# Latent attention on one core: outputs copied out by ScalarE and added by GpSimd, query blocks in another order

## The chip, the cores and the metric

One core of a Trainium2 chip. Times are device microseconds of one execution; the kernel before took 740.17 us in the median of 3 runs (739.23 to 742.46). One more execution was taken with a profile; all rows of the trace are from it.

## What is computed

One layer for 1024 tokens of width 1024, with 16 heads: multi-head latent attention, a gate on its output, an output projection, then a gated per-layer embedding and a last norm. Cut to what matters here:

```python
u = rmsnorm(x, norm_g) @ w_in            # 384 | 256 | 32 | 1024 columns: c_q, c_kv, k_rope, z
q = rmsnorm(c_q, q_norm) @ w_q_b         # 16 heads of 64 + 32 (rotary)
k_nope, v = split(rmsnorm(c_kv, kv_norm) @ w_kv_b)   # 16 heads of 64 + 64
for blk in range(8):                     # query blocks of 128 tokens
    s = (q_nope @ k_nope.T + rope(q_rope) @ rope(k_rope).T) * scale   # keys up to the block's end
    prob = softmax(where(k_chunk <= q_chunk, s, -inf))                # chunks of 64
    o[blk] = prob @ v
x = x + (o * silu(z)) @ w_out
gate = sigmoid(rmsnorm(x) @ ple_gate)
out = rmsnorm(x + gate * (p @ ple_proj), final_norm)
```

Every product is made of three matmuls of split operands (high x high, high x low, low x high): each operand is stored as a rounded high part and the low part that is left.

## The kernel before, in words

The program is written for a scheduler that orders each engine's instructions ahead of time; on the chip every engine works off its own list in order, and waits at each instruction for what that one needs. The stages:

- Up to 69 us: `u_tile` projects the tokens to the latent queries and keys (`cq_hi`, `cq_lo`, `ckv_hi`, `ckv_lo`).
- 69 to 181 us, the gate projection: the loop over `c` (L500). Each round makes 48 matmuls of `z` for 128 features (L510) from weights that come through the one staging buffer `zs` (`z_weights`, L344: high part `zh` on ScalarE L357, low part `zl` on VectorE L358). Rounds 2 to 5 also project the rotary parts of four heads' queries (`project_r`, L421): 18 matmuls (L417) with `wrh` and `wrl`, the split rotary weights; four products with cosine and sine on VectorE (L429); a copy of the high part on ScalarE (L431); the low part on GpSimd (L432, a subtraction made by the helper `sub_hi`, L91); four DMAs issued by GpSimd (L434). The rotary weights come from `weights_r` (L496), which calls `load_split` (L391): a DMA on SP's queue into one of two buffers `ws`, the high part `hi` (L397) and the low part `lo` (L398, shown as L91), both on GpSimd. The weights of queries, keys and values (`wq`, `wk`, `wv`) go the same way.
- 181 to 517 us, attention, head after head. For each head and query block `scores` (L597) makes the scores in PSUM, masks 64x64 of them (L611), takes the row maximum on VectorE (L613) and the exponential on ScalarE (L618) into `prob`. Blocks over 512 columns use one of two buffers of two banks (`ps_big`), smaller ones one of four buffers of one bank (`ps_tr`), which they share with transposes, projections and outputs. `prob_transposes` (L640) turns the probabilities in TensorE, 128x128 at a time (L118); ScalarE copies the high parts out of PSUM (L656), VectorE the low parts (L657, shown as L91). `values` (L659) multiplies them with the values, once for the blocks 4 to 7 of a head (16 long matmuls' group, `pt1`) and once for the blocks 0 to 3 (`pt0`). The product of the high values stands in one half of the partitions and that of the low values in the other; ScalarE copies one half to `o` (L671), VectorE adds the other half from PSUM (L672), GpSimd multiplies with the gate in `zT` (L674), in the last two heads VectorE.
- The order of the work in attention is a list of head and block (L690); `ORDER` (L37) gives the blocks of a head and `LAST` (L38) those of the last one. The projections of coming heads are put between blocks by tables of positions: `V_FIRST`, `V_AT` for values, `K_AT` for keys, `Q_AT` for queries (L40, L41). Transposes follow 2 blocks behind the scores (`LAG`), outputs 4 (`LAGV`). After each odd head `normalise` (L621) scales the gate by the reciprocal sums. The scheduler makes each engine's list from these positions, so moving one of them moves instructions on all engines.
- From 517 us: output projection and embedding, mostly the matmuls of L757.

Of the kernel before, what the change touches and what calls it, by code (L numbers as in the profile page):

```python
# [9 lines left out]
F32 = mybir.dt.float32  # L10
# [4 lines left out]
ALU = mybir.AluOpType  # L15
AX = mybir.AxisListType

P = 128
# [4 lines left out]
H = 16  # L23
QL = 384
# [9 lines left out]
INV_FREQ = [10000.0 ** (-2.0 * i / ROPE) for i in range(ROPE // 2)]  # L34
HF = ROPE // 2
ROUND = 12582912.0
ORDER = (7, 0, 6, 1, 5, 2, 4, 3)  # L37
LAST = (7, 0, 6, 1, 5, 2, 3, 4)  # L38
WARM = 9
V_FIRST = (1, 1, 5, 3)  # L40
V_AT, K_AT, Q_AT, ROPE_AT = (5, 5, 3, 3), (1, 3), (7, 5), 4  # L41
LAG, LAGV, LEAD, ODD_AT = 2, 4, 2, 1
TWO_PI = 2.0 * math.pi

# [7 lines left out]
def mla_ple_kernel(ctx, tc, x, x_t, p_t, pos, norm_g, w_c, w_z, q_norm, w_q, w_r, kv_norm, w_k, w_v,  # L52
# [7 lines left out]
    V, A, G = nc.vector, nc.scalar, nc.gpsimd  # L60
# [6 lines left out]
    def ps_big():  # L67
        return psum.tile([P, 1024], F32, tag="big", name="ps_big", bufs=2)

    def ps_tr():  # L70
        return psum.tile([P, 512], F32, tag="one", name="ps_tr", bufs=4)
# [18 lines left out]
    def sub_hi(eng, lo, src, hi):  # L90
        eng.tensor_tensor(out=lo, in0=src, in1=hi.bitcast(F32), op=ALU.subtract)  # L91
# [45 lines left out]
    def rh_tile(name):  # L137
        return both.tile([P, S], F32R, tag="rh", name=name, bufs=1)
# [9 lines left out]
    ps = ps_tr()  # L148
# [238 lines left out]
    att1 = late.enter_context(pool("att1", side="right"))  # L387
    att2 = late.enter_context(pool("att2", side="right"))
    k_hi, k_lo = zip(*([att2.tile([P, S], F32R, name=f"k_{z}{e}") for z in ("hi", "lo")] for e in range(2)))

    def load_split(src, cols, name, bufs, home=att1):  # L391
        n = math.prod(cols)
        stg = att1.tile([P, 512], F32, tag="ws", name="ws", bufs=2)[:, :n]
        nc.sync.dma_start(out=stg, in_=src)
        hi = home.tile([P, n], F32R, tag=name + "h", name=name + "h", bufs=bufs)
        lo = home.tile([P, n], F32R, tag=name + "l", name=name + "l", bufs=bufs)
        G.tensor_copy(out=hi, in_=stg)  # L397
        sub_hi(G, lo, stg, hi)  # L398
        return tuple(z.rearrange("p (k n) -> p k n", k=cols[0]) for z in (hi, lo))

    wk_of, wv_of, wq_of, q_of, rq_of = {}, {}, {}, {}, {}
# [91 lines left out]
    zw = zph.enter_context(pool("zw", reuse_waits="tile"))  # L493
    cs = [zw.tile([P, S], F32, name=f"cs{e}") for e in range(2)]

    def weights_r(g):  # L496
        return load_split(w_r[g], (QL // P, P), "wr", 1, zw)


    for c in range(KT):  # L500
# [36 lines left out]
    pt = [[att.tile([P, 16 * g + 10, P], F32R, name=f"pt{g}{z}") for z in "hl"] for g in range(2)]  # L537
    vals = att.tile([P, NT, 2, 4, VD], F32R, name="vals")
    kst = {}

    def prob_tile():
        return att.tile([P, S], F32, tag="prob", name="prob", bufs=3)
# [54 lines left out]
    def scores(h, i):  # L597
        e = h % 2
        q = q_of[h]
        qs = slice(i * P, (i + 1) * P)  # L600
        n = (i + 1) * P
        off = P if n == 640 else 0
        spans = {128: [(0, 256)], 640: [(0, 384), (384, 640)]}.get(
            n, [(a, min(a + 512, n)) for a in range(0, n, 512)])
        ps = ps_big() if n > 512 else ps_tr()
        for s0, s1 in spans:
            for a, b in pairs:
                nc.tensor.matmul(ps[:, off + s0:off + s1], q[a][:, qs], (k_hi, k_lo)[b][e][:, s0:s1],  # L608
                                 start=a + b == 0, stop=a == 1)
        s = ps[:, off:off + n]  # L610
        V.memset(s[0:64, n - 64:], MASKED)  # L611
        mx = small.tile([P, 1], F32, tag="mx", name="mx")
        V.tensor_reduce(out=mx, in_=s, axis=AX.X, op=ALU.max, negate=True)  # L613
        pr = prob_tile()
        if e == 0 and i == order(h)[0]:
            sums[h // 2] = small.tile([P, 2 * NT], F32, tag="l", name="l", bufs=2)
        l = sums[h // 2][:, e * NT + i:e * NT + i + 1]
        A.activation(out=pr[:, :n], in_=s, func=AF.Exp, bias=mx, scale=1.0, accum_out=l)  # L618
        return pr
# [39 lines left out]
    def values(h, g):  # L659
# [9 lines left out]
        top, bot = slice(e * VD, (e + 1) * VD), slice((1 - e) * VD, (2 - e) * VD)  # L669
        o = att.tile([P, 512], F32, tag="o1", name="o1", bufs=2)  # L670
        A.copy(out=o[top], in_=ps[bot])  # L671
        V.tensor_tensor(out=o[top], in0=ps[top], in1=o[top], op=ALU.add)  # L672
        z = zT[top, c, g * 512:(g + 1) * 512]
        (V if h >= H - 2 else G).tensor_tensor(out=z, in0=o[top], in1=z, op=ALU.mult)  # L674

# [226 lines left out]
```

## Time and profile before

| | before |
|---|---|
| runs, median (lowest to highest) | 740.17 us (739.23 to 742.46) |
| the profiled execution | 742.71 us |
| its span, first to last instruction | 740.9 us |
| TensorE busy | 712.6 us (96%) |
| VectorE busy | 525.6 us (71%) |
| ScalarE busy | 401.2 us (54%) |
| GpSimd busy | 209.2 us (28%) |
| granted TensorE clock, mean | 0.989 of full speed |

Time in the trace counts from the span's start. In the profile PE is TensorE, PEld its weight loads, DVE VectorE, ACT ScalarE, POOL GpSimd, SP SyncE, whose queue issues most DMAs. Matmuls overlap, so a matmul's duration is longer than the step from one to the next; the step is the cost. An idle time is put down to what ended it last. `L91` is a helper's line that many subtractions share; the tile names tell them apart.

### The profile page before, as it was taken

The numbers are of one execution on the slowest core, as the hardware profiler recorded it, in microseconds if no ns is written. First come the engines' busy times: TensorE is split into PE (matmuls) and PEld (weight loads), VectorE is DVE, ScalarE is ACT, GpSimd is POOL, SyncE is SP. The second block draws the span as 40 slices with busy tenths as digits, with TensorE's granted clock in tenths as the row PEclk, the third lists the DMA queues.
The fourth block names the chain that finished last, engine by engine and source line by source line (L and its number), as shares of the span: only waits on it lengthen the run. The fifth ranks groups of instructions, "written<-read, shape, count | busy, mean of one in ns | idle before, by whom it ended". The sixth has DMA issues, their size and how long they took to land.

```text
span 740.9 us, 11048 instructions
## 1 busy us (share of the span) xinstructions
PE 712.6 (96%) x3776; PEld 599.2 (81%) x3776; DVE 525.6 (71%) x1270; ACT 401.2 (54%) x921; POOL 209.2 (28%) x204
## 2 busy tenths in 40 slices
PE   8999999979999999999999999999999999999995
PEld 7999888858887778878888788877768887888885
DVE  6995456641887787888788887888555239788854
ACT  6752344331777676777777776776443135243322
POOL 0004316670223232323324232156136132000000
PEclk9999999989999999999999999999999999999998
DMA  8812524462311212101121211033384021110101
GB/s 310 286 56 68 132 77 176 164 216 76 85 44 29 76 30 75 39 27 56 30 75 44 76 29 47 13 115 85 116 297 128 0 86 28 37 43 36 58 28 58
DMA packets 27191, 63.90 MB, mean 86 GB/s; under 512 B 4600, under 2 KB 9088, under 8 KB 27136
## 3 DMA queue, kind: packets, MB, share of 16 engines
q1 hardware_dynamic: 23312, 52.05, 22.6%
q0 software_dynamic: 3536, 11.02, 4.4%
q8 instruction: 30, 0.49, 0.3%
q14 instruction: 25, 0.20, 0.1%
q10 hardware_dynamic: 288, 0.14, 0.1%
HBM read 50.01 MB, written 13.18 MB: 85 GB/s over the span
## 4 chain that ended last, share of the span: by engine, by line
PE 69%; DVE 11%; ACT 8%; issue 4%; DMA 3%; POOL 3%; SPq 0%; ACTq 0%; DVEq 0%; POOLq 0%
PE ps_big L757 17%; PE ps_big L510 9%; PE ps_o L667 9%; PE ps_tr L118 6%; PE ps_big L608 5%; PE ps_pj L417 4%; PE ps_big L212 3%; PE ps_pj L569 3%; PE ps_pj L550 3%; ACT prob L618 3%; DVE pt1l L91 3%; PE ps_pj L757 3%; PE ps_big L213 3%; PE ps_tr L608 2%; DVE mx L613 2%
## 5 line engine op out<-in xcount | busy, mean ns | idle before, releaser
L757 PE MATMUL ps_big<-w,aTh 128*128 128x512 f32 (+1 forms) x480 | 140.2, 392 | 1.8 <-ACT sg L833 1.8
L757 PEld LDWEIGHTS ps_big<-w,aTh 128*128 128x128 f32 x480 | 90.1, 189 | 22.2 <-ACT sg L833 2.2
L118 PE MATMUL ps_tr<-ident,prob 128*128 128x128 f32 x576 | 84.6, 275 | 6.0 <-ACT prob L618 3.3
L757 PE MATMUL ps_big<-w,aTl 128*128 128x512 f32 (+1 forms) x240 | 85.1, 392 | 0.6 <-POOL aTl L91 0.5
L118 PEld LDWEIGHTS ps_tr<-ident,prob 128*128 128x128 f32 x576 | 66.5, 140 | 20.6 <-ACT prob L618 10.2
L674 POOL TENSOR_TENSOR zT<-o,zT 64x512 f32<-64x512 f32 x28 | 36.0, 1287 | 141.2 <-DVE o L672 141.1
L91 DVE TENSOR_TENSOR pt1l<-ps_tr,pt1h 128x512 fp32r<-128x512 f32 (+1 forms) x144 | 72.7, 536 | 3.9 <-ACT pt1h L656 2.5
L656 ACT CAST pt1h<-ps_tr 128x512 fp32r<-128x512 f32 (+1 forms) x144 | 62.0, 470 | 24.2 <-PE ps_tr L118 12.0
L618 ACT ACTIVATE prob<-ps_big,mx 128x1024 f32<-128x1024 f32 (+1 forms) x64 | 61.3, 958 | 18.3 <-DVE mx L613 17.1
L613 DVE TENSOR_REDUCE mx<-ps_big 128x1 f32<-128x1024 f32 (+1 forms) x64 | 64.9, 1015 | 0.3
L358 DVE SCALAR_TENSOR_TENSOR zl<-zs,g_col,zh 128x128 fp32r<-128x128 f32 x56 | 31.3, 607 | 32.9 <-ACT zh L357 32.6
L757 PEld LDWEIGHTS ps_big<-w,aTl 128*128 128x128 f32 x240 | 45.3, 189 | 11.4 <-POOL aTl L91 1.5
L608 PE MATMUL ps_big<-k_hi,qh 128*128 128x512 f32 (+2 forms) x128 | 48.6, 380 | 0.0
L608 PE MATMUL ps_big<-k_hi,ql 128*128 128x512 f32 (+2 forms) x128 | 46.5, 363 | 0.0
L608 PE MATMUL ps_big<-k_lo,qh 128*128 128x512 f32 (+2 forms) x128 | 46.1, 360 | 0.0
L357 ACT ACTIVATE zh<-zs,g_col 128x128 fp32r<-128x128 f32 x56 | 18.3, 392 | 50.2 <-DMA zs<-in_w_z 47.2
L667 PE MATMUL ps_o<-pt1h,vals 128*128 128x512 f32 (+3 forms) x128 | 42.9, 361 | 1.5 <-DVE pt1l L91 1.0
L113 ACT ACTIVATE jk<-xs 128x512 bf16<-128x512 f32 (+2 forms) x25 | 18.7, 750 | 42.3 <-DVE xs L835 35.1
L667 PE MATMUL ps_o<-pt1l,vals 128*128 128x512 f32 (+3 forms) x128 | 41.6, 363 | 0.0
L672 DVE TENSOR_TENSOR o<-ps_o,o 64x512 f32<-64x512 f32 x32 | 22.0, 688 | 25.3 <-ACT o L671 25.2
L618 ACT ACTIVATE prob<-ps_tr,mx 128x128 f32<-128x128 f32 (+1 forms) x64 | 33.8, 529 | 5.5 <-DVE mx L613 5.3
L91 DVE TENSOR_TENSOR pt0l<-ps_tr,pt0h 128x128 fp32r<-128x128 f32 (+2 forms) x80 | 33.2, 416 | 4.5 <-ACT pt0h L656 2.9
(289 smaller groups left out, 1806.7 us busy)
## 6 DMA issues: line engine op xcount, KB each, us to landing
zT<-in_x SPq DMA_DIRECT2D x8, 512.0 KB, 4.5
rlb<-rl SPq DMA_DIRECT2D x32, 128.0 KB, 3.0
wst<-in_w_out SPq DMA_DIRECT2D x8, 512.0 KB, 4.1
xs<-in_x SPq DMA_DIRECT2D x8, 512.0 KB, 7.0
wst<-in_ple_gate SPq DMA_DIRECT2D x8, 512.0 KB, 3.7
zs<-in_w_z SPq DMA_DIRECT2D x14, 256.0 KB, 2.9
out<-xs SPq DMA_DIRECT2D x14, 256.0 KB, 2.0
zT<-in_x_t SPq DMA_DIRECT2D x6, 512.0 KB, 3.7
```

The source lines that it names most:

```text
L91: eng.tensor_tensor(out=lo, in0=src, in1=hi.bitcast(F32), op=ALU.subtract)
L118: nc.tensor.transpose(dst[:, j * P:(j + 1) * P], src[:, j * P:(j + 1) * P], ident)
L358: V.scalar_tensor_tensor(out=lo[:, k, :], in0=stg[:, k, :], scalar=g, in1=hi[:, k, :].bitcast(F32), op0=ALU.mult, op1=ALU.subtract)
L417: nc.tensor.matmul(ps, w[b][:, k, :], (cq_hi, cq_lo)[a][:, k, hf * 512:hf * 512 + 512], start=k == 0 and a + b == 0, stop=k == n - 1 and a ...
L510: nc.tensor.matmul(ps[:, hf * 512:(hf + 1) * 512], wz[b][:, k % 4, :], (hT_hi, hT_lo)[a][:, k, hf * 512:(hf + 1) * 512], start=k == 0 and ...
L608: nc.tensor.matmul(ps[:, off + s0:off + s1], q[a][:, qs], (k_hi, k_lo)[b][e][:, s0:s1], start=a + b == 0, stop=a == 1)
L613: V.tensor_reduce(out=mx, in_=s, axis=AX.X, op=ALU.max, negate=True)
L618: A.activation(out=pr[:, :n], in_=s, func=AF.Exp, bias=mx, scale=1.0, accum_out=l)
L656: A.copy(out=hi, in_=src[:, ks])
L667: nc.tensor.matmul(ps[:, q * P:], vals[:, j, c % 2, 2 * e:2 * e + 2, :], pt[g][n][:, at:at + 4 - q, :], start=j + n == 0, stop=(j, n) == ( ...
L674: (V if h >= H - 2 else G).tensor_tensor(out=z, in0=o[top], in1=z, op=ALU.mult)
L757: nc.tensor.matmul(o, st[a][:, k, :], w[k][b][:, cols], start=k == 0 and a + b == 0, stop=k == nk - 1 and a == 1)
```

## The change

Five edits. `load_split` takes the engine of the high and the low part as arguments, and the rotary weights now use ScalarE and VectorE in place of GpSimd. Scores of 256 to 512 columns use `ps_big` too; only those of 128 columns keep `ps_tr`. In the heads before the last two, ScalarE copies the second half of an output out as well, into a tile `o_hi` of its own, and GpSimd adds the two. The blocks of a head go 7, 6, 0, 1, 5, 4, 2, 3, in the last head 7, 6, 3, 2, 1, 0, 5, 4. The positions of the projections of values, keys and queries are other ones. Behind line 540 the change has one line more than the kernel before (its L609 is L608 there, L614 is L613, L668 is L667), and behind the new adds in `values` six more in all (its L763 is L757).

```diff
@@ -34,11 +34,11 @@
 INV_FREQ = [10000.0 ** (-2.0 * i / ROPE) for i in range(ROPE // 2)]
 HF = ROPE // 2
 ROUND = 12582912.0
-ORDER = (7, 0, 6, 1, 5, 2, 4, 3)
-LAST = (7, 0, 6, 1, 5, 2, 3, 4)
+ORDER = (7, 6, 0, 1, 5, 4, 2, 3)
+LAST = (7, 6, 3, 2, 1, 0, 5, 4)
 WARM = 9
-V_FIRST = (1, 1, 5, 3)
-V_AT, K_AT, Q_AT, ROPE_AT = (5, 5, 3, 3), (1, 3), (7, 5), 4
+V_FIRST = (1, 2, 4, 6)
+V_AT, K_AT, Q_AT, ROPE_AT = (6, 7, 4, 5), (4, 5), (7, 6), 4
 LAG, LAGV, LEAD, ODD_AT = 2, 4, 2, 1
 TWO_PI = 2.0 * math.pi
 
@@ -388,14 +388,14 @@
     att2 = late.enter_context(pool("att2", side="right"))
     k_hi, k_lo = zip(*([att2.tile([P, S], F32R, name=f"k_{z}{e}") for z in ("hi", "lo")] for e in range(2)))
 
-    def load_split(src, cols, name, bufs, home=att1):
+    def load_split(src, cols, name, bufs, home=att1, copy=G.tensor_copy, eng=G):
         n = math.prod(cols)
         stg = att1.tile([P, 512], F32, tag="ws", name="ws", bufs=2)[:, :n]
         nc.sync.dma_start(out=stg, in_=src)
         hi = home.tile([P, n], F32R, tag=name + "h", name=name + "h", bufs=bufs)
         lo = home.tile([P, n], F32R, tag=name + "l", name=name + "l", bufs=bufs)
-        G.tensor_copy(out=hi, in_=stg)
-        sub_hi(G, lo, stg, hi)
+        copy(out=hi, in_=stg)
+        sub_hi(eng, lo, stg, hi)
         return tuple(z.rearrange("p (k n) -> p k n", k=cols[0]) for z in (hi, lo))
 
     wk_of, wv_of, wq_of, q_of, rq_of = {}, {}, {}, {}, {}
@@ -494,7 +494,7 @@
     cs = [zw.tile([P, S], F32, name=f"cs{e}") for e in range(2)]
 
     def weights_r(g):
-        return load_split(w_r[g], (QL // P, P), "wr", 1, zw)
+        return load_split(w_r[g], (QL // P, P), "wr", 1, zw, A.copy, V)
 
 
     for c in range(KT):
@@ -537,6 +537,7 @@
     pt = [[att.tile([P, 16 * g + 10, P], F32R, name=f"pt{g}{z}") for z in "hl"] for g in range(2)]
     vals = att.tile([P, NT, 2, 4, VD], F32R, name="vals")
     kst = {}
+    o_hi = rh_tile("o_hi").bitcast(F32)
 
     def prob_tile():
         return att.tile([P, S], F32, tag="prob", name="prob", bufs=3)
@@ -602,7 +603,7 @@
         off = P if n == 640 else 0
         spans = {128: [(0, 256)], 640: [(0, 384), (384, 640)]}.get(
             n, [(a, min(a + 512, n)) for a in range(0, n, 512)])
-        ps = ps_big() if n > 512 else ps_tr()
+        ps = ps_big() if n > P else ps_tr()
         for s0, s1 in spans:
             for a, b in pairs:
                 nc.tensor.matmul(ps[:, off + s0:off + s1], q[a][:, qs], (k_hi, k_lo)[b][e][:, s0:s1],
@@ -669,7 +670,12 @@
         top, bot = slice(e * VD, (e + 1) * VD), slice((1 - e) * VD, (2 - e) * VD)
         o = att.tile([P, 512], F32, tag="o1", name="o1", bufs=2)
         A.copy(out=o[top], in_=ps[bot])
-        V.tensor_tensor(out=o[top], in0=ps[top], in1=o[top], op=ALU.add)
+        if h >= H - 2:
+            V.tensor_tensor(out=o[top], in0=ps[top], in1=o[top], op=ALU.add)
+        else:
+            o2 = o_hi[top, g * 512:(g + 1) * 512]
+            A.copy(out=o2, in_=ps[top])
+            G.tensor_tensor(out=o[top], in0=o2, in1=o[top], op=ALU.add)
         z = zT[top, c, g * 512:(g + 1) * 512]
         (V if h >= H - 2 else G).tensor_tensor(out=z, in0=o[top], in1=z, op=ALU.mult)
 
```

What the change moves on an engine's list shows at three places. First GpSimd in the third round with rotary queries of the gate projection, between the weights of attention and the DMAs of the rotated queries (`rq2h`, `rq2l` are their DRAM tiles; `rt`, `rh` and parts of `zT` hold their low and high parts). Before:

```order
L397 CAST wrh<-ws 128x384
L397 CAST wvh<-ws 128x512
L91 TENSOR_TENSOR zT<-zT 128x1024
L434 DMA rq2h<-zT 128x2x512
L434 DMA rq2l<-zT 128x2x512
L91 TENSOR_TENSOR rt<-rt,rh 128x1024
L434 DMA rq2h<-rh 128x2x512
L434 DMA rq2l<-rt 128x2x512
L91 TENSOR_TENSOR wrl<-ws,wrh 128x384
L91 TENSOR_TENSOR wvl<-ws,wvh 128x512
```

With the change:

```order
L91 TENSOR_TENSOR wvl<-ws,wvh 128x512
L91 TENSOR_TENSOR zT<-zT 128x1024
L434 DMA rq2h<-zT 128x2x512
L434 DMA rq2l<-zT 128x2x512
L91 TENSOR_TENSOR rt<-rt,rh 128x1024
L434 DMA rq2h<-rh 128x2x512
L434 DMA rq2l<-rt 128x2x512
L91 TENSOR_TENSOR zT<-zT 128x1024
```

The copies and subtractions of `wrh` and `wrl` are gone from GpSimd; before, `wrl` stood behind both subtractions of the rotated queries and their four DMAs, and the low part of the value weights behind it.

Second VectorE in an even head of attention, around the first outputs of the head before it. Before, from the low parts of the probabilities of a small block on:

```order
L91 TENSOR_TENSOR pt0l<-ps_tr,pt0h 128x3x128
L91 TENSOR_TENSOR pt0l<-ps_tr,pt0h 128x128
L672 TENSOR_TENSOR o_3242<-ps_o,o_3242 64x512
L91 TENSOR_TENSOR pt1l<-ps_tr,pt1h 128x4x128
L91 TENSOR_TENSOR pt1l<-ps_tr,pt1h 128x3x128
L611 MEMSET ps_tr 64x64
L613 TENSOR_REDUCE mx<-ps_tr 128x1
L91 TENSOR_TENSOR pt1l<-ps_tr,pt1h 128x128
```

With the change:

```order
L91 TENSOR_TENSOR pt0l<-ps_tr,pt0h 128x3x128
L91 TENSOR_TENSOR pt1l<-ps_tr,pt1h 128x4x128
L91 TENSOR_TENSOR pt0l<-ps_tr,pt0h 128x128
L91 TENSOR_TENSOR pt1l<-ps_tr,pt1h 128x3x128
L612 MEMSET ps_big 64x64
L614 TENSOR_REDUCE mx<-ps_big 128x1
L91 TENSOR_TENSOR pt1l<-ps_tr,pt1h 128x128
L612 MEMSET ps_big 64x64
```

The add of the output (L672), which waited for ScalarE's copy and stood ahead of the low parts of block 7, is gone from the list.

Third TensorE in an even head, at its scores of blocks 6, 0 and 5 before, and 0, 1 and 5 with the change, with the engines that each instruction waits for in brackets (Activation is ScalarE). Before:

```order
L608 MATMUL ps_big<-k_hi_967,qh 128x384
L608 MATMUL ps_big<-k_lo_968,qh 128x384
L608 MATMUL ps_big<-k_hi_967,ql 128x384
L608 MATMUL ps_tr<-k_hi_967,qh 128x256 [waits DVE_49]
L608 MATMUL ps_tr<-k_lo_968,qh 128x256
L608 MATMUL ps_tr<-k_hi_967,ql 128x256
L608 MATMUL ps_big<-k_hi_967,qh 128x512 [waits Activation_49]
L608 MATMUL ps_big<-k_lo_968,qh 128x512
```

With the change:

```order
L609 MATMUL ps_tr<-k_hi_967,qh 128x256 [waits PE_49]
L609 MATMUL ps_tr<-k_lo_968,qh 128x256
L609 MATMUL ps_tr<-k_hi_967,ql 128x256
L118 MATMUL ps_tr<-ident,prob 128x128 [waits DVE_49,Activation_49]
L118 MATMUL ps_tr<-ident,prob 128x128 x3
L609 MATMUL ps_big<-k_hi_967,qh 128x256
L609 MATMUL ps_big<-k_lo_968,qh 128x256
L609 MATMUL ps_big<-k_hi_967,ql 128x256
L609 MATMUL ps_big<-k_hi_967,qh 128x512 [waits Activation_49]
L609 MATMUL ps_big<-k_lo_968,qh 128x512
```

Block 1 (256 columns) takes a large buffer with the change, and block 5 then waits for the exponential of ScalarE that frees the other; before, large and small blocks took turns in buffers of two kinds.

## Rows read from the trace of the kernel before

**Rows 1.** Busy time by stage: stretch, length, then PE, PEld, DVE, ACT, POOL busy, clock.
```profile
297.66:381.86 84.20, 82.74 (x496) 70.54 (x495) 69.71 (x155) 62.31 (x153) 27.37 (x24) 1.00 0.17 50
```

**Rows 2.** Chain that ended last, in order of time, attention: start us, us, what.
```profile
297.66 3.10 PE ps_o L667 x16
...
319.60 3.40 PE ps_o L667 x16
...
336.96 3.10 PE ps_o L667 x16
...
381.86 3.12 PE ps_o L667 x16
```

**Rows 3.** Waits, gate projection: who, for whom, us in total, times, longest.
```profile
PE ps_pj L417 <- POOL wrl L91: 4.9, 1, 4.9
```

**Rows 4.** Timeline of GpSimd around that wait: start us, us, what, idle before.
```profile
145.17 2.40 POOL L91 TENSOR_TENSOR zT<-zT 128x1024 fp32r<-128x1024 f32 x1
...
148.98 2.35 POOL L91 TENSOR_TENSOR rt<-rt,rh 128x1024 fp32r<-128x1024 f32 x1
...
152.73 1.00 POOL L91 TENSOR_TENSOR wrl<-ws,wrh 128x384 fp32r<-128x384 f32 x1
```

**Rows 5.** Timeline of TensorE's matmuls at that wait.
```profile
153.79 0.80 PE L417 MATMUL ps_pj<-cq_hi,wrl 128*128 128x512 f32 x1 [4.92 <-POOL wrl L91]
...
157.80 0.42 PE L417 MATMUL ps_pj<-cq_hi,wrl 128*128 128x512 f32 x1
158.05 0.39 PE L417 MATMUL ps_pj<-cq_lo,wrh 128*128 128x512 f32 x1
158.28 0.40 PE L417 MATMUL ps_pj<-cq_hi,wrh 128*128 128x512 f32 x1
```

**Rows 6.** Busy time by stretch, around that wait.
```profile
150.00:155.00 5.00, 1.21 (x3) 1.02 (x4) 2.63 (x2) 0.00 (x0) 4.94 (x5) 0.60 0.79 255
```

**Rows 7.** Timeline of VectorE, third round: the last products with cosine and sine.
```profile
140.92 1.28 DVE L429 TENSOR_TENSOR rt<-ps_pj,cs 128x512 f32<-128x512 f32 x2
```

**Rows 8.** Instructions by form, whole span: count, busy us, mean ns, idle before.
```profile
L674 POOL TENSOR_TENSOR zT<-o,zT 64x512 f32<-64x512 f32 x28 | 36.0, 1287 | 141.2 <-DVE o L672 141.1
L671 ACT COPY o<-ps_o 64x512 f32<-64x512 f32 x32 | 18.6, 581 | 13.7 <-PE ps_o L667 12.4 <-POOL wkl L91 1.1
L672 DVE TENSOR_TENSOR o<-ps_o,o 64x512 f32<-64x512 f32 x32 | 22.0, 688 | 25.3 <-ACT o L671 25.2
```

**Rows 9.** Chain that ended last: the gate matmuls between two rounds.
```profile
107.52 10.91 PE ps_big L510 x48
```

**Rows 10.** Waits of TensorE's weight loads, attention (205 to 500 us).
```profile
PEld ps_tr L118 <- ACT prob L618: 5.9, 12, 1.1
...
PEld ps_tr L608 <- DVE o L672: 1.8, 7, 0.4
PEld ps_pj L550 <- DVE o L672: 1.5, 7, 0.3
...
PEld ps_pj L569 <- DVE o L672: 0.9, 3, 0.3
PEld ps_o L667 <- DVE o L672: 0.9, 3, 0.3
```

**Rows 11.** The tile zl: VectorE's instructions, ns least, median, most.
```profile
L358 DVE SCALAR_TENSOR_TENSOR zl<-zs,g_col,zh x56: 336/350/3401, 72.2 to 167.0; 128x128 fp32r<-128x128 f32 x56
```

**Rows 12.** Timeline of one large score block: last matmul, read of the sums.
```profile
312.94 0.39 PE L608 MATMUL ps_big<-k_hi,ql 128*128 128x512 f32 x1
...
317.30 0.20 ACT L618 ACTIVATION_READ_ACCUMULATOR prob<-ps_big,mx 128x1 f32 x1
```

**Rows 13.** Instructions by form, whole span: maxima and exponentials.
```profile
L613 DVE TENSOR_REDUCE mx<-ps_big 128x1 f32<-128x1024 f32 x16 | 19.4, 1212 | 0.0
...
L618 ACT ACTIVATE prob<-ps_big,mx 128x1024 f32<-128x1024 f32 x16 | 17.9, 1118 | 2.4 <-DVE mx L613 2.3
...
L613 DVE TENSOR_REDUCE mx<-ps_tr 128x1 f32<-128x256 f32 x16 | 6.7, 422 | 0.4
```

## The prediction

> **What bounds the kernel now.** I read the busy times by stage first, then the waits of one stage at a time, then the instructions around the longest wait. In the attention stage [rows 1] four heads take 84.20 us: TensorE is busy for 82.74 of it, VectorE for 69.71, ScalarE for 62.31, GpSimd for 27.37. So TensorE bounds this stage, VectorE is next at 83%, ScalarE at 74%, and GpSimd has two thirds of its time free. That the stretch is four heads is seen in the chain [rows 2]: the sixteen long output matmuls of a head start at 297.66, 319.60, 336.96, once more, and at 381.86. A head takes 21.05 us on average; the shortest takes 17.36 us.
>
> The one long hole of TensorE lies earlier, in the gate projection. There it waits 4.9 us, once, for `wrl`, the low part of a rotary weight that GpSimd writes [rows 3]. GpSimd's own rows [rows 4] say why: it starts on the low part of a rotated query at 145.17, goes through two such subtractions of about 2.4 us and four DMA issues, and reaches `wrl` only at 152.73. TensorE's rows [rows 5] show what it costs: the matmul at 153.79 starts after 4.92 us of idle time, so the hole began at 148.87. The granted clock reads 0.60 of full speed in the five microseconds around the hole [rows 6], a mix of its two levels, and from 153.79 to 157.80 ten matmul starts lie some 0.43 us apart (1.2 GHz) instead of the 0.23 that follows (2.4 GHz). So 9 x 0.233 = 2.1 us of work took 4.0, another 1.9 us.
>
> **The change part by part.**
>
> Rotary weights: their high part goes to ScalarE and their low part to VectorE. GpSimd loses the work that TensorE waited for, and the new order has `wrl` right behind the four products of VectorE that read the same projection; GpSimd's rotated queries no longer stand ahead of it. In the third round the last pair of those products ran from 140.92 to 142.20 [rows 7], against TensorE's need at 148.87. The price on the new engines: ScalarE's copy of 64x512 takes 0.581 us and VectorE's add of 64x512 takes 0.688 us [rows 8]; the new ones have 384 elements per lane, so they cost at most that, four times: 2.3 and 2.8 us, and at least nothing, since both lie under the 10.9 us of gate matmuls between two rounds [rows 9]. If that cover is gone, TensorE waits again. Taken: all of the hole goes, 4.9 + 1.9 = **-6.8 us**. The bounds are 0 (another wait takes its place) and -6.8. On the SP queue the rotary weights wait for VectorE to free their staging buffer instead of GpSimd, and one of them moves ahead of two gate weights; the weights of queries, keys and values keep their place behind it. GpSimd casts these three ahead of its third pair of rotated queries, now with all low parts before it: some 1.3 us more there, if a subtraction of 512 elements per lane takes what its product of 512 takes [rows 8], off TensorE's path.
>
> Outputs: for 14 of 16 heads VectorE loses 28 adds, 28 x 0.688 = 19.3 us, and the waits for ScalarE's copy ahead of them, 25.3 us over the kernel [rows 8]. ScalarE gains 28 copies, 28 x 0.581 = 16.3 us, some 1.2 us in a head, where it has 5.5 us free [rows 1]. GpSimd gains 28 adds at the 1.287 us of its product of the same size [rows 8]: 36.0 us, 2.6 in a head, where 14.2 are free. No matmul reads these products before the last stage; but the low keys of the odd head and the weights of the next pair of heads queue behind the adds, 2.6 us later at the worst, which is little against the head that lies between them and their use. The gain is read from what TensorE's weight loads waited for with this add as the last releaser, since the add's end frees the PSUM bank [rows 10]: 1.8 + 1.5 + 0.9 + 0.9 = **-5.1 us**. Its bounds: 0, if the loads' waits were hidden under running matmuls; -11.0, if the 5.9 us of waits for an exponential go too, VectorE being free earlier for the maxima ahead of them. I take 5.1, because the idle time of TensorE in four heads, 84.20 - 82.74 = 1.46 us, times four is 5.8, the nearest to it.
>
> Block order, projections, PSUM: the matmuls are the same in number and shape, so TensorE's own work is unchanged. The scores of 256 to 512 columns leave the four one-bank buffers for the two large ones. The cost of this is not in the trace; its bounds are 0 and the price in the slower rival below. I take 0, for the reason given there. The DMAs of weights move with the projections and stay a head ahead of their use.
>
> Last head: its order now ends on blocks 5 and 4. It may add or save one wait for an exponential, at the longest 1.1 us [rows 10]; I take 0.
>
> Sum: -6.8 - 5.1 = -11.9 us. The profiled execution took 742.7 us (span 740.9 and 1.8 around it), so 730.8 us against its own time. The median of the runs shown, 740.2, is 2.5 us lower; against that the forecast is **728.3 us**.
>
> A rule that speaks against the first part. The row: the 56 low parts of the gate weights on VectorE, 128x128, take 0.336 us at the least, 0.350 in the median and 3.401 at the longest [rows 11]; the long ones lie beside GpSimd's 2.4 us subtractions [rows 4]. The Trainium skill, "SBUF — State Buffer", section "Who interferes with whom", says that a VectorE instruction with two SBUF inputs and a GpSimd instruction that reads SBUF exclude each other for a whole instruction. By that rule `wrl`, both of whose inputs are in SBUF, would pay one GpSimd subtraction more on VectorE, each of four times; under the cover it would cost nothing, and the trace agrees as far as the long rows go.
>
> **The rivals.**
>
> Slower: the two large score buffers become the bound. A block holds its buffer from its first matmul to the end of its exponential. For 1024 columns that is six matmuls at 0.23, a maximum of 1.21, an exponential of 1.12 and a read of 0.20, 3.9 us; for 256 columns some 1.5 (three short matmuls 0.4, a maximum of 0.42, about as much for the exponential, 0.2) [rows 12, 13]. Seven blocks at the mean of 2.7 make 18.9 us. Two buffers offer 42.1 us in a head, so each block may queue for (42.1 - 18.9) / 7 = 3.3 us. In the trace a block of 1024 columns has its last matmul at 312.94 and is read out at 317.50, 4.6 us, of which 2.5 is work: 2.0 us of queueing. From 3.3 us on, each 0.1 us costs 0.35 us per head, 5.6 us in 16 heads, and above 3.5 us it eats all gains. At 3.6 us: 740.2 - 6.8 + 16.8 = 750 us. For it: ScalarE has more in its queue, and in the shortest head the allowance is only (34.7 - 18.9) / 7 = 2.3 us. Against it: the average head has 1.3 us to spare, and VectorE's queue gets shorter.
>
> Only the hole goes: TensorE had other work whenever the add was late, and the waits turn into waits for exponentials. For it: 1.46 us of idle time in 84. Then 740.2 - 6.8 = 733.4 us.
>
> The waits for exponentials go as well: 728.3 - 5.9 = 722.4 us. For it: VectorE has 1.4 us less work per head and no wait for ScalarE's copy; against it: ScalarE, which does the exponentials, has more.
>
> The hole stays, so that this part of the change doesn't do what it says: `wrl` is held on VectorE behind products that wait for the rotated queries' DMAs, or by GpSimd's subtractions, for longer than the 6.7 us between 142.2 and 148.9. One subtraction is 2.4 us, so it would take three. Then 740.2 - 5.1 = 735.1 us.
>
> **How the numbers follow.** Forecast 0.56; only the hole goes 0.15; exponentials too 0.12; the hole stays 0.06; slower 0.11. The range of 720 to 738 us takes in the first four with 2 to 3 us of their own spread and leaves out the slower rival and a better case than any named. A measurement of this kernel can tell about 0.5%, 3.7 us, from no change. Faster by more than that (under 736.5) are nearly all of the first four, 0.81; within it a part of the second and fourth and a mild form of the slower one, 0.10; slower 0.09.
>
> **What would show it.** Right: no wait of TensorE on `wrl` and full granted clock from 140 to 180 us; the attention stage starting some 7 us earlier; no weight load waiting for an add of outputs; four heads in about 83 us; VectorE near 64 us in them, ScalarE near 67. Wrong: first score matmuls that wait for ScalarE, or heads longer than 21 us, would show the score buffers as the bound; a hole of TensorE around 149 us with VectorE as releaser would show that the wait only changed hands.

## The result, and the profile after

The changed kernel took 750.5 us in the median of three runs (748.7 to 751.8), against 740.2 before: a ratio of 1.012, with an interval of 1.010 to 1.014. It is slower, and far above the forecast of 728.3 and its range.

The profiled execution has a span of 750.0 us, 9.1 more than before. Two rows of its busy times by stage say where that was won and lost (columns as in [rows 1]):

```profile
140.00:160.00 20.00, 20.00 (x89) 16.46 (x88) 11.31 (x18) 8.67 (x16) 13.58 (x13) 1.00 0.52 174
```
```profile
313.96:401.79 87.83, 82.63 (x495) 70.69 (x495) 65.87 (x147) 66.24 (x160) 37.29 (x33) 1.00 0.17 48
```

Around the old hole TensorE is now busy for 20.00 of 20 us, at full granted clock; [rows 3] and [rows 6] have no counterpart any more. That is the forecast's first gain. The second row is four heads, from the long output matmuls of one head to those of the fourth after it: 87.83 us, where [rows 1] had 84.20. TensorE's own work in it is the same (82.63 against 82.74), so the 3.6 us are waits. VectorE fell to 65.87, ScalarE rose to 66.24 and GpSimd to 37.29, all near what was forecast, and yet the heads are longer. Read over the whole span, the first long output matmul of the first head starts 9.2 us earlier (201.20 against 210.43), that of the last head 11.2 us later (535.03 against 523.86), and the rest takes 2.1 us less (215.0 against 217.1). So the 15 steps from head to head lost 20.4 us in all. At 3.6 us in four heads that would be some 14 (an estimate); the rest lies mainly in the first step (24.90 against 22.14), in the last (23.47 against 19.00) and in TensorE's clock, below.

The waits of the attention stage (205 to 515 us: who, for whom, us in total, times, longest) show what TensorE now waits for:

```profile
PE ps_big L609 <- ACT prob L619: 15.8, 19, 1.6
PE ps_tr L118 <- ACT o_hi L677: 3.5, 11, 0.5
```
```profile
PEld ps_big L609 <- ACT prob L619: 22.3, 26, 1.8
PEld ps_tr L118 <- ACT o_hi L677: 8.3, 14, 0.7
```

First: a score matmul that needs one of the two large buffers waits for the exponential that still reads it. Before, this wait stood in the stage once, for 0.2 us, in a weight load. Second: transposes wait for the bank of an output, which ScalarE's new copy releases. Before, weight loads waited for VectorE's add of the outputs, 5.1 us in all [rows 10]; that wait changed hands and grew.

The two longest of these waits, 1.6 and 1.5 us, lie in heads with no projections (2, 6 and 10; in head 14 they are 1.0 and 1.2). This is the timeline of head 6 (start us, us, engine, line, what, idle before):

```profile
323.18 0.42 PE L609 MATMUL ps_big<-k_hi,qh 128*128 128x384 f32 x1
...
324.42 1.15 DVE L91 TENSOR_TENSOR pt1l<-ps_tr,pt1h 128x512 fp32r<-128x512 f32 x2
...
325.01 0.94 ACT L619 ACTIVATE prob<-ps_big,mx 128x768 f32<-128x768 f32 x1
...
326.09 0.44 PE L609 MATMUL ps_big<-k_hi,qh 128*128 128x384 f32 x1 [1.56 <-ACT prob L619]
326.12 0.80 DVE L614 TENSOR_REDUCE mx<-ps_big 128x1 f32<-128x640 f32 x1
...
326.72 0.82 PE L118 MATMUL ps_tr<-ident,prob 128*128 128x128 f32 x6
...
327.35 0.86 ACT L657 CAST pt1h<-ps_tr 128x512 fp32r<-128x512 f32 x2 [1.32 <-PE ps_tr L118]
...
328.10 0.81 ACT L619 ACTIVATE prob<-ps_big,mx 128x640 f32<-128x640 f32 x1
...
328.79 0.21 ACT L619 ACTIVATION_READ_ACCUMULATOR prob<-ps_big,mx 128x1 f32 x1
...
329.06 0.50 PE L609 MATMUL ps_big<-k_hi,qh 128*128 128x512 f32 x1 [1.52 <-ACT prob L619]
```

The block of 640 columns takes its buffer at 323.18 and gives it back at 329.00: 5.8 us. Of these some 2.9 are work (matmuls until 324.3, maximum 0.80, exponential 0.81, read 0.21) and 2.9 are queueing: the maximum stands behind low parts on VectorE, the exponential behind casts on ScalarE. And the wait feeds itself. The score matmul at 326.09 stands ahead of six transposes on TensorE; they start at 326.72, so ScalarE idles 1.32 us for them, casts them, and only then comes to the exponential for which the next score matmul waits, 1.52 us more.

A smaller part is TensorE's clock. Busy times around the same place in head 10, and TensorE's two waits there:

```profile
402.00:415.60 13.60, 11.52 (x74) 9.69 (x72) 9.60 (x23) 10.20 (x25) 5.74 (x6) 1.00 0.13 33
415.60:422.40 6.80, 5.52 (x17) 4.44 (x18) 3.31 (x9) 3.33 (x10) 2.29 (x2) 0.50 0.54 142
```
```profile
413.92 0.44 PE L609 MATMUL ps_big<-k_hi,qh 128*128 128x384 f32 x1 [1.57 <-ACT prob L619]
...
416.88 0.79 PE L609 MATMUL ps_big<-k_hi,qh 128*128 128x512 f32 x1 [1.52 <-ACT prob L619]
```

The same two waits are joined here by 6.80 us at a granted clock of 0.50 (1.2 GHz); the second score matmul takes 0.79 us instead of the 0.50 above. From output matmuls to output matmuls head 6 took 19.38 us and head 10 took 21.97, 2.6 us more for the clock:

```profile
313.96:333.34 19.38, 16.04 (x99) 13.58 (x98) 14.26 (x33) 14.01 (x35) 7.98 (x7) 1.00 0.21 61
401.79:423.76 21.97, 18.61 (x99) 15.55 (x99) 14.48 (x33) 14.07 (x36) 8.24 (x7) 0.84 0.25 64
```

### The profile page after: what moved, and what is told of

The parts are those of the page before. It is cut to its first block, busy times and chain, and to the rows that moved or that the text cites. A ratio compares the mean times of both kernels' runs of the same rounds, so it can differ in the third digit from the quotient of the medians.

```text
span 750.0 us, 11038 instructions
## 1 busy us (share of the span) xinstructions
PE 712.9 (95%) x3776; PEld 603.0 (80%) x3776; DVE 516.6 (69%) x1246; ACT 415.9 (55%) x953; POOL 238.1 (32%) x224
## 5 line engine op out<-in xcount | busy, mean ns | idle before, releaser
L763 PE MATMUL ps_big<-w,aTh 128*128 128x512 f32 (+1 forms) x480 | 139.2, 390 | 0.6 <-ACT sg L839 0.6
L619 ACT ACTIVATE prob<-ps_big,mx 128x1024 f32<-128x1024 f32 (+6 forms) x112 | 90.0, 803 | 35.7 <-DVE mx L614 34.9
L763 PEld LDWEIGHTS ps_big<-w,aTh 128*128 128x128 f32 x480 | 89.3, 188 | 20.6 <-ACT sg L839 1.0
L118 PE MATMUL ps_tr<-ident,prob 128*128 128x128 f32 x576 | 89.3, 279 | 7.9 <-ACT o_hi L677 3.5
L614 DVE TENSOR_REDUCE mx<-ps_big 128x1 f32<-128x1024 f32 (+6 forms) x112 | 91.8, 820 | 2.3
L609 PE MATMUL ps_big<-k_hi,qh 128*128 128x512 f32 (+2 forms) x176 | 71.1, 404 | 16.8 <-ACT prob L619 16.6
L763 PE MATMUL ps_big<-w,aTl 128*128 128x512 f32 (+1 forms) x240 | 84.4, 389 | 0.0
L91 DVE TENSOR_TENSOR pt1l<-ps_tr,pt1h 128x512 fp32r<-128x512 f32 (+2 forms) x144 | 75.0, 537 | 13.3 <-ACT pt1h L657 12.2
L678 POOL TENSOR_TENSOR o<-o_hi,o 64x512 f32<-64x512 f32 x28 | 35.9, 1283 | 128.6 <-ACT o_hi L677 128.5
L657 ACT CAST pt1h<-ps_tr 128x512 fp32r<-128x512 f32 (+3 forms) x144 | 63.6, 472 | 13.9 <-PE ps_tr L118 9.0
L609 PE MATMUL ps_big<-k_hi,ql 128*128 128x512 f32 (+2 forms) x176 | 64.3, 366 | 0.0
L609 PE MATMUL ps_big<-k_lo,qh 128*128 128x512 f32 (+2 forms) x176 | 62.8, 357 | 0.0
L609 PEld LDWEIGHTS ps_big<-k_hi,qh 128*128 128x128 f32 x176 | 33.6, 191 | 26.7 <-ACT prob L619 23.6
L763 PEld LDWEIGHTS ps_big<-w,aTl 128*128 128x128 f32 x240 | 45.1, 188 | 10.0
L668 PE MATMUL ps_o<-pt1h,vals 128*128 128x512 f32 (+3 forms) x128 | 41.5, 350 | 0.0
L668 PE MATMUL ps_o<-pt1l,vals 128*128 128x512 f32 (+3 forms) x128 | 41.5, 363 | 0.0
```

Source lines behind the costliest of these rows:

```text
L118: nc.tensor.transpose(dst[:, j * P:(j + 1) * P], src[:, j * P:(j + 1) * P], ident)
L657: A.copy(out=hi, in_=src[:, ks])
L668: nc.tensor.matmul(ps[:, q * P:], vals[:, j, c % 2, 2 * e:2 * e + 2, :], pt[g][n][:, at:at + 4 - q, :], start=j + n == 0, stop=(j, n) == ( ...
L678: G.tensor_tensor(out=o[top], in0=o2, in1=o[top], op=ALU.add)
L763: nc.tensor.matmul(o, st[a][:, k, :], w[k][b][:, cols], start=k == 0 and a + b == 0, stop=k == nk - 1 and a == 1)
```

## The experiments

Parts of the change were taken out of the changed kernel, and parts were put alone into the kernel before. Each time comes with its difference in us to the median of the runs of before on the same chip (740.4 to 741.3), the ratio of the two and the 95% interval of the ratio. The changed kernel itself was timed only in the three runs above, beside a before of 740.2 us; differences to its 750.5 us are between chips, and before alone differs by up to 1.2 us between these.

**Taking parts out of the changed kernel.** The first theory was the prediction's slower rival, the score buffers. Score line undone:

```
-        ps = ps_big() if n > P else ps_tr()
+        ps = ps_big() if n > 512 else ps_tr()
```

> The changed kernel with one line undone: scores of 256 to 512 columns go to the four one-bank buffers again. Theory (two score buffers bound the heads, which cost about 16 us after the gate stage had gained 7): most of the 16 us comes back, 733 to 738 us, four heads in about 84 us instead of 88, and nearly no wait of a first score matmul for an exponential. Rival 1 (ScalarE's and GpSimd's added work on the outputs delays the exponentials): 748 to 752 us. Rival 2 (the block order is worse by itself): 748 to 752 us.

Measured 755.8 us (+14.6; 1.021, 1.017 to 1.026). The theory in this form fell, and the time lies above its rivals' too: the waits at the large buffers went (0.6 us are left), and worse ones came. TensorE's waits in the stage:

```profile
PE ps_tr L609 <- DVE k_lo L91: 4.7, 7, 0.7
PE ps_tr L118 <- ACT prob L619: 4.6, 6, 0.8
PE ps_tr L609 <- DVE pt1l L91: 3.1, 4, 0.8
PE ps_pj L551 <- ACT prob L619: 2.4, 7, 0.5
```

Now the four one-bank buffers are short: scores wait for a bank that held a key projection (`k_lo`) or transposes (`pt1l`) until VectorE had read it.

Outputs undone (the add back on VectorE, `o_hi` and the copy into it gone):

> The changed kernel with the outputs' add back on VectorE and the second copy of ScalarE gone. Theory (score buffers): the buffers are still two, 747 to 755 us, four heads in 87 to 89 us. Rival 1 (the added work on ScalarE delays the exponentials): 733 to 738 us, heads of 84 us. Rival 2 (block order): 747 to 755 us.

Measured 743.4 us (+2.3; 1.001, 0.999 to 1.004), between the theory and its rival: 7 us come back, so this edit costs too, against the theory.

Orders and places undone:

```
-ORDER = (7, 6, 0, 1, 5, 4, 2, 3)
-LAST = (7, 6, 3, 2, 1, 0, 5, 4)
+ORDER = (7, 0, 6, 1, 5, 2, 4, 3)
+LAST = (7, 0, 6, 1, 5, 2, 3, 4)
...
-V_FIRST = (1, 2, 4, 6)
-V_AT, K_AT, Q_AT, ROPE_AT = (6, 7, 4, 5), (4, 5), (7, 6), 4
+V_FIRST = (1, 1, 5, 3)
+V_AT, K_AT, Q_AT, ROPE_AT = (5, 5, 3, 3), (1, 3), (7, 5), 4
```

> The changed kernel with both block orders and the places of the projections as before. Theory (score buffers): blocks of 256 to 512 columns still share the two large buffers, so 744 to 752 us, heads of 86 to 88 us on four. Rival 2 (block order): 733 to 738 us. Rival 1 (ScalarE's added work): 748 to 752 us.

Measured 739.7 us (-1.5; 0.998, 0.997 to 1.000): 11 us come back, nearest to rival 2.

**Each part alone.** The score line alone in the kernel before:

> The kernel before with only the one line on the score buffers changed: 256 to 512 columns into the two large ones. Theory: slower by the 16 us lost, 750 to 758 us, with four heads in 87 us or more and the first score matmuls waiting for exponentials. Rivals 1 and 2 (ScalarE's added work, or the block order): 738 to 743 us.

Measured 744.2 us (+3.0; 1.005, 1.003 to 1.007): slower, but not by 16.

The rotary weights' part alone (`copy=A.copy, eng=V` for `wr`):

> The kernel before with only the rotary weights' parts moved to ScalarE and VectorE. Theory (the gate stage's gain is real and the loss lies in the heads): the first term of the prediction alone, 732 to 736 us, no wait for the low rotary weight. Rival (the scheduler's new sort of the engines gives the gain back in the heads): 738 to 743 us.

Measured 732.9 us (-8.4; 0.990, 0.986 to 0.994), and nothing of it is given back: the first long output matmuls of a head start 6.7 us earlier, and so do the last.

The outputs' edit alone:

> The kernel before with only the outputs' edit: two copies by ScalarE, the add by GpSimd. Theory now (the block order with its places is what costs, and the outputs' edit costs only on top of it, since undoing either gave 7 to 11 us): 737 to 742 us in the old order. Rival (28 more copies on ScalarE cost the same 7 us in any order, because exponentials queue behind them): 746 to 749 us. The prediction's own term: 735 us.

Measured 746.3 us (+4.9; 1.007, 1.005 to 1.010): the rival's time. Orders and places alone:

> The kernel before with only the two block orders and the places of the projections. Theory now (the order is worse by itself: with the score line undone the changed kernel still took 755.8 us): 748 to 756 us, four heads in 88 to 90 us. Rival (it costs only together with ScalarE's added copies): 739 to 745 us.

Measured 751.2 us (+9.9; 1.013, 1.009 to 1.018). So far the four parts add up, -8.4 + 4.9 + 9.9 + 3.0 = +9.4, to about what all of them did; but undoing the score line had shown that they act on each other. Next, the places alone taken out of the changed kernel:

> The changed kernel with the places of the projections as before, the block orders still new (7, 6, 0, 1, 5, 4, 2, 3). If the places cost the time (the projections stand in the second half of a head and leave its first half without cover): 738 to 743 us. If the order of the blocks does (two large blocks one behind the other): 747 to 755 us.

Measured 752.8 us (+11.5; 1.014, 1.009 to 1.019). With the other edits there, the old places give nothing back. (Its four runs took 746.7 to 753.5 us; the rows of this run further down are from the fastest, whose mean granted clock was 0.995, against 0.986 and 0.987 in the others.) Now the line on the score buffers undone in the heads without projections only:

```
-        ps = ps_big() if n > P else ps_tr()
+        ps = ps_big() if n > (512 if h % 4 == 2 else P) else ps_tr()
```

> The changed kernel, with the score line undone only in the heads 2, 6, 10 and 14, which have no projection to cover a wait. Theory (in these four heads the two large buffers are the bound: two waits of about 1.7 us each, and one stretch at half clock behind them; in the others the line does no harm): 738 to 746 us, and the two waits gone. Rival (the line must be undone everywhere or nowhere, since the one-bank buffers are then short, as in the run that undid it everywhere, 755.8 us): 749 to 756 us.

Measured 746.7 us (+5.8; 1.008, 1.005 to 1.011), between the two. The two long waits went. At full granted clock such a head took 18.18 us (head 10), against 19.38 in the changed kernel; head 6 took 19.74, with a part of it at half clock (columns as before):

```profile
404.01:422.19 18.18, 16.24 (x98) 13.50 (x98) 13.32 (x32) 13.50 (x35) 7.23 (x7) 1.00 0.17 51
315.97:335.71 19.74, 17.79 (x98) 14.86 (x98) 13.33 (x32) 13.59 (x35) 7.98 (x7) 0.91 0.15 46
```

So undoing the line wins 1.2 us in such a head; before, it took 17.12. The weight loads of head 6 now wait for one-bank buffers (311 to 334 us):

```profile
PEld ps_tr L118 <- ACT o_hi L677: 1.1, 2, 0.8
PEld ps_tr L609 <- PE ps_tr L118: 1.1, 1, 1.1
```

With this order TensorE waits at either set of buffers.

**Why the outputs' edit costs.** The second copy made by VectorE:

```
-            A.copy(out=o2, in_=ps[top])
+            V.tensor_copy(out=o2, in_=ps[top])
```

> The kernel before with the outputs' add on GpSimd and the second copy made by VectorE instead of ScalarE, so that ScalarE's queue is as before. Theory (the 28 copies on ScalarE are what cost 4.9 us, since exponentials and casts queue behind them): 738 to 742 us. Rival (the add's way over GpSimd, or any new sort of the engines, costs the same): 744 to 748 us.

Measured 742.7 us (+1.8; 1.003, 1.001 to 1.004), between the two and nearer the theory: with the copy on another engine 3.1 of the 4.9 us are gone. And ScalarE's copies without the rest of the edit (28 copies that nothing reads are added, the add stays on VectorE):

> The kernel before with ScalarE's 28 added copies alone; nothing reads them, and the add stays on VectorE. Theory (the copies cost because exponentials and casts queue behind them on ScalarE): 744 to 749 us, at least the 4.9 us that the outputs' edit cost. Rival (ScalarE has room for 16 us of copies, and the edit costs by the add's way over GpSimd): 740 to 742 us.

Measured 757.2 us (+15.9; 1.024, 1.021 to 1.027), more than three times what the edit cost and far above the theory's range. Four heads of the outputs' edit, of VectorE's copy and of the added copies, in this order (same columns):

```profile
297.13:383.48 86.35, 82.72 (x498) 70.81 (x496) 64.72 (x147) 66.66 (x161) 37.50 (x32) 1.00 0.18 48
```
```profile
298.59:382.78 84.19, 82.73 (x498) 70.51 (x496) 69.68 (x155) 62.29 (x153) 37.48 (x32) 1.00 0.18 50
```
```profile
303.92:393.89 89.97, 85.65 (x497) 70.71 (x495) 69.21 (x155) 66.48 (x161) 27.34 (x24) 1.00 0.17 46
```

With 10 us more on GpSimd and ScalarE as before, the heads take 84.19 us, to a hundredth those of [rows 1]: GpSimd's part is free in them. (The 1.8 us of that run lie elsewhere; in its profile the step from the 15th head's long output matmuls to the 16th's takes 20.94 us, against 19.00 before.) With 4.2 us more on ScalarE alone they take 5.8 more. In the edit 2.2 remain, perhaps because VectorE has 5 us less to do; no run separates that. So ScalarE's idle time is not room here. That it lies inside a chain is the likely reason: the waits of ScalarE in the stage, in the outputs' edit, are led by

```profile
ACT prob L619 <- DVE mx L614: 20.2, 44, 1.1
ACT o L672 <- PE ps_o L668: 13.5, 19, 0.9
```

waits for its predecessors; what is put ahead of an exponential or a cast in its queue would move all that follows. The rows do not show this step by step. TensorE's own longest wait in the outputs' edit names VectorE, not one of the copies:

```profile
PE ps_tr L609 <- DVE pt0l L91: 6.3, 8, 0.9
```

The low part `pt0l` stands there behind the maximum of a block of 1024 columns (in head 6 the maximum starts at 316.01 and `pt0l` at 317.75 us; before, at 314.59 and 316.66), in a list that the scheduler sorted anew. And in the run with the added copies alone these hold the output's bank 0.58 us longer ahead of the add, and of the 5.8 us in four heads 2.9 are in TensorE's busy time (85.65 against 82.74), so not all of the 15.9 us need be ScalarE's queue.

**The last head's order** undone in the changed kernel:

> The changed kernel with only the last head's order as before. The prediction's term is 0: 748 to 752 us. By the traces the stretch from the last head but one to the end is 229.6 us in the changed kernel and 226.3 where both orders are the old ones; if the last head's order does it: 746 to 748 us.

Measured 749.1 us (+8.2; 1.012, 1.010 to 1.014), 1.4 less than the 750.5, inside its spread: the term of 0 stands.

**Why the orders cost.** Block orders alone, and places alone:

> The kernel before with only the two block orders, the places of the projections as before. If the order of the blocks is what costs: 748 to 753 us, like order and places together (751.2). If the places do: 739 to 743 us, and no wait of 1.2 us behind the key projections of the odd heads.

> The kernel before with only the places of the projections, the block orders as before. If the places cost (key projections at the fifth and sixth block, where their banks wait for VectorE behind a maximum): 747 to 752 us with a wait of about 1.2 us in each odd head. If the block order does: 739 to 743 us.

Measured 739.9 us (-1.3; 0.998, 0.996 to 1.000) and 751.7 (+10.4; 1.015, 1.013 to 1.018). In the old order it is the places. A wait of that run, once in each odd head but the last (7 times, 8.1 us):

```profile
322.33 1.21 DVE L613 TENSOR_REDUCE mx<-ps_big 128x1 f32<-128x1024 f32 x1
...
323.57 0.69 DVE L91 TENSOR_TENSOR ql<-ps_pj,qh 64x512 fp32r<-64x512 f32 x1
...
324.32 0.65 PE L118 MATMUL ps_tr<-ident,prob 128*128 128x128 f32 x4 [1.18 <-DVE ql L91]
```

The query projections now stand at the last two blocks of a head, beside the next head's block of 1024 columns. VectorE's low part of the queries, which frees the projection's bank, stands behind that block's maximum, and TensorE waits 1.18 us for the bank. (The expectation had named the key projections.) Before, only weight loads waited there, 0.2 us at the longest; with orders and places both new, scores wait for the bank of a key projection instead:

```profile
PEld ps_tr L118 <- DVE ql L91: 1.1, 7, 0.2
```
```profile
PE ps_tr L608 <- DVE k_lo L91: 7.2, 7, 1.0
```

But the old places did not help the changed kernel, so one more edit had to turn the new block order into a cost:

> The kernel before with the block orders and the score line only. If the two edits add: 739.9 + 3.0 = 743 us. If they act on each other (the new order sets two of the longest blocks side by side, 7 and 6, 5 and 4, and both large score buffers are then held for long): 747 to 752 us, with two waits of over 1.5 us in each head without projections.

> The kernel before with the block orders and the outputs' edit only. If the two edits add: 739.9 + 4.9 = 745 us. If ScalarE's added copies are what makes the new block order a cost: 749 to 754 us.

Measured 754.8 us (+14.4; 1.019, 1.016 to 1.023) for block orders and score line, and 745.4 (+5.0; 1.007, 1.004 to 1.009) for block orders and outputs. The outputs' edit adds its 5 us; the score line, +3.0 in the old order, costs 14.9 in the new one (754.8 - 739.9). That is more than the expectation's range, and its sign is missing: the heads 2, 6 and 10 have one wait of over 1 us each, of some 1.2, not two of over 1.5. Four heads of the score line alone, of the block orders alone, and of both:

```profile
297.67:382.98 85.31, 81.27 (x495) 70.65 (x495) 70.50 (x155) 63.05 (x153) 27.18 (x24) 1.00 0.18 49
```
```profile
295.40:379.54 84.14, 82.30 (x496) 70.18 (x494) 69.70 (x155) 62.57 (x153) 27.29 (x24) 1.00 0.18 49
```
```profile
299.86:387.27 87.41, 83.08 (x496) 70.71 (x496) 70.23 (x155) 62.75 (x153) 27.34 (x24) 1.00 0.17 48
```

87.41 us, nearly the changed kernel's 87.83, with VectorE's, ScalarE's and GpSimd's work as before. The waits of this run in the stage are the changed kernel's too:

```profile
PE ps_big L608 <- ACT prob L618: 13.5, 21, 1.5
PE ps_tr L118 <- DVE o L672: 2.3, 7, 0.3
```

But the score line brings nearly as much of the first of these in the old order, where it costs 3.0 us:

```profile
PE ps_big L608 <- ACT prob L618: 11.3, 12, 1.4
```

In four heads TensorE's idle time (length less busy time) grows with the line by 2.6 us in the old order (1.46 to 4.04) and by 2.5 in the new one (1.84 to 4.33). What differs is its busy time, for as many matmuls: it falls by 1.5 us with the line in the old order (82.74 to 81.27) and grows by 0.8 in the new one (82.30 to 83.08). So the waits at the large buffers are the line's own cost, in either order, and why the new order makes it dearer is not shown by them. In the old order a short block (0, 1, 2) stands between the long ones; in the new one 7 and 6, and 5 and 4, are neighbours, so that both large buffers are held by long blocks when the next score needs one. That is an argument, and the rows do not bear it out.

And the places? Four heads of orders and places without the score line, of the changed kernel with the outputs undone, and of the changed kernel with the old places:

```profile
297.63:384.36 86.73, 83.68 (x495) 70.39 (x495) 71.06 (x155) 61.34 (x152) 27.35 (x24) 1.00 0.17 48
```
```profile
378.16:463.15 84.99, 81.74 (x495) 70.93 (x495) 69.66 (x156) 62.80 (x152) 27.44 (x24) 1.00 0.16 45
```
```profile
291.46:379.31 87.85, 83.03 (x496) 70.76 (x494) 65.94 (x147) 66.00 (x160) 37.49 (x32) 1.00 0.16 47
```

Without the score line the new places add 2.6 us (86.73 against 84.14). With it they take 2.4 off (84.99 against 87.41; the rotary weights' part, too, differs between these two), and with the outputs' edit there as well they change nothing (87.83 against 87.85). The waits say why in part: without the line scores and transposes wait for a bank that holds a projection (`ql` 8.1 us with the places alone, `k_lo` 7.2 with orders and places, and 4.7 in the changed kernel with the line undone); with it the small scores leave these banks, and the list of the changed kernel has no such row.

**Versions that beat both.** The rotary weights' part with the score line in odd heads only, and with the block orders:

> The kernel before with the rotary weights' part, and the score line changed in the odd heads only. In the run with the line everywhere the odd heads took 21.5 us against 22.2 and the others more. Theory (the line helps where a head has projections of its own to cover the queueing): 8 x 0.7 = 5.6 us less than the 732.9 us of the rotary part alone, 726 to 730 us. Rival (what an odd head gains is only shifted to its neighbours): 732 to 737 us.

> The kernel before with the rotary weights' part and the block orders: if they add, 732.9 - 1.3 = 731 to 733 us, the fastest of all; if not, 734 to 740 us.

Measured 735.2 us (0.993, 0.991 to 0.995): what odd heads won, their neighbours lost; and 733.0 (0.990, 0.987 to 0.993). The rotary part alone, 732.9, is as good, and simpler: that is what to keep of this change.

## Why the prediction was wrong, by its steps

**The hole, -6.8 us: right.** Alone it gave 8.4 in the medians, with an interval of 4.7 to 10.7, and the heads start 6.7 us earlier. The cover was there. The Trainium skill ("SBUF — State Buffer", section "Who interferes with whom") would have let `wrl` on VectorE take a GpSimd subtraction longer. This case's trace agrees: its four instructions took 0.553 us at the least and 2.481 at the longest, the two long ones beside GpSimd's subtractions of 2.4 us, and no engine waited for them.

```profile
L91 DVE TENSOR_TENSOR wrl<-ws,wrh x4: 553/1510/2481, 75.8 to 142.7; 128x384 fp32r<-128x384 f32 x4
```

**The outputs, -5.1 us: wrong in sign, +4.9.** The step that failed is "ScalarE gains 28 copies ... some 1.2 us in a head, where it has 5.5 us free". A share of busy time was taken for room. Four heads grew by 5.8 us when only ScalarE's copies were added. The step on GpSimd's adds, priced at nothing, was right in the heads. The gain was mis-sized as well: the 5.1 us were waits of weight loads, and these overlap matmuls (70.54 us of loads and 82.74 of matmuls lie in the 84.20 us of [rows 1]). Of the matmuls in the stage (205 to 500 us) one waited for this add, before:

```profile
PE ps_tr L608 <- DVE o L672: 0.2, 1, 0.2
```

So there was next to nothing to win from this wait; 0 was the term's lower bound. And the weight loads' waits did not go: they wait for ScalarE's copy instead of VectorE's add.

**Block order, projections, PSUM, 0: the main miss.** The block orders alone are indeed 0, and the last head's order too. The places alone are +10.4, and "The DMAs of weights move with the projections and stay a head ahead of their use" looked at the weights, not at the banks that projections hold until VectorE comes to them. The score line is +3.0 in the old order and +14.9 in the new. In the changed kernel these do not add: the new places make no difference there that the runs can tell (750.5 against 752.8 us, on two chips; four heads 87.83 against 87.85).

**The slower rival**, with a chance of 0.11, had one of the mechanisms, its place and its sign: first score matmuls that wait for ScalarE, and heads longer than 21 us. That its time, 750 us, was met is luck: it put all 16.8 us on the score buffers, while the line costs 3.0 alone, undoing it in the changed kernel made that slower (755.8), and the outputs and the places, which it left at nothing, cost 4.9 and 10.4 alone. What spoke against it, "the average head has 1.3 us to spare", was an error: heads cannot lend each other buffers. The prediction's own allowance for the shortest head was 2.3 us a block (and its 17.36 us is 17.12 by the first long matmul, 319.60 to 336.72); the block shown above queued 2.9. With the block orders alone such a head took 18.16 us, with the score line added 20.16:

```profile
316.99:335.15 18.16, 17.61 (x103) 14.67 (x104) 14.83 (x35) 13.21 (x36) 6.22 (x6) 1.00 0.26 71
```
```profile
321.66:341.82 20.16, 17.59 (x105) 14.67 (x104) 16.75 (x37) 13.99 (x35) 5.96 (x5) 1.00 0.26 70
```

The rival also left out that the waiting score matmul holds up transposes behind it.

What stays open: why the score line costs more in the new block order; by which way ScalarE's copies reach TensorE; and why the new places gain with the score line and no longer with the outputs' edit as well. Every edit lets the scheduler sort all engines' queues anew; the runs do not separate that from the buffers.

## What to carry to other kernels

Price a change of buffers at the stretch with the least cover, and with the order of work that the change itself brings: how long each holder keeps its buffer there, queueing included. Before an engine's free time is used, ask what that time is waiting for: idle time inside a chain of small steps (score, maximum, exponential, transpose, cast) need not be room. Here 28 copies of 0.58 us, 16 us of work, made the kernel 15.9 us slower. A wait of a weight load is not a wait of the matmuls; price a gain by the latter. Test the parts of a bundle alone and in pairs: here one part was worth 8 us, and the others together lost 17.6 (750.5 - 732.9).

## What was not expected

The same pair of waits (1.6 and 1.5 us within some three microseconds) left the granted clock at 1.00 in the heads 2 and 6 and came with 6.80 us at 0.50 in head 10, 90 us later in the same execution. So such a pair can have a second price, here 2.6 us, that comes at some of its places and not at others.
